# Three of four chunks of each down projection as seven products of quarters

## The chip, the cores and the metric

The kernel runs on one core of one Trainium2 chip, in one launch. The metric is the device time of one execution in microseconds. The core has five engines that run their own queues in strict order and wait for each other by semaphores: TensorE (PE, matrix products into PSUM), VectorE (DVE), ScalarE (ACT), GpSimd (POOL) and SyncE (SP, whose queue issues every DMA of this kernel).

## The reference

A trunk of two layers over 512 tokens with 1024 features: a token mixer, an MLP with 4096 hidden features, and a gated embedding, each added to the residual x. Only the MLP is touched:

```python
def sq_relu_mlp(h, w_up, w_down):
    return jnp.square(jax.nn.relu(h @ w_up)) @ w_down
...
        x = x + sq_relu_mlp(rmsnorm(x, mlp_norm[i]), w_up[i], w_down[i])
        gate = jax.nn.sigmoid(rmsnorm(x, ple_norm[i]) @ w_ple_gate[i])
        x = x + gate * (p[i] @ w_ple_proj[i])
    return rmsnorm(x, final_norm)
```

## The kernel before

Features lie on the 128 partitions and the 512 tokens (S) along the free axis, so x is 8 tiles of 128 x 512. Every operand of a product is held as two parts, hi (rounded to the matmul's type) and lo (the rest). mm3 (L161) makes a product from three matmuls, hi x hi, lo x hi and hi x lo (L163 to L165): in dense (L273) the weights are the stationary operand and the activations the moving one of 512 columns. split (L167) makes the two parts: ACT casts (L170), DVE subtracts (L171).

Weights come in blocks of 128 x 1024 in the order of _schedule, which is also their order in memory. fetch (L125) brings one: SP issues the DMA into a raw tile wr (L137), ACT casts it to wh (L138), DVE subtracts for wl (L139). The three tags have three buffers each, and load (L142) keeps two blocks ahead of PE. A cast into wh therefore waits until PE is done with the block three places earlier.

mlp (L643) goes through the hidden features in four chunks of 1024. An up projection of a chunk is 8 dense blocks (24 matmuls each, 8 tiles of the contraction x 3) whose results DVE takes through relu and the norm's row factor (L659), ACT squares (L660) and split makes into operands. A down projection of a chunk is again 8 dense blocks, one for each 128 output features, with the chunk's 8 hidden tiles as moving operands; residual (L285) adds each result to x. The up blocks of chunk c + 1 stand partly before and partly after the down blocks of chunk c. In the last chunk the norm of the gate takes each finished tile of x (nG.tile), which POOL adds up (L236).

A scheduler places the instructions of each engine by priority and by the buffers that it thinks free, so the order on an engine is not simply the order of the code. PSUM has eight banks; hf has 18 buffers of 128 x 512, ar has 24 of 128 x 1024, qk three of 128 x 4 x 416.

Of the kernel before, what the change touches and what calls it, by code (L numbers as in the profile page):

```python
# [15 lines left out]
F32 = mybir.dt.float32  # L16
# [7 lines left out]
P = 128  # L24
# [15 lines left out]
G_A, G_B, G_MLP, G_PLE, G_FIN, G_Q, G_KV, G_N = 0, 8, 16, 32, 48, 56, 58, 59  # L40


def _schedule():

    out = []
    for i in range(GH):
        out += [(("qkv", i, b), 1024) for b in range(4)]
        if i == 0:
            out += [(("v0", b), n * 320) for b, n in enumerate((3, 3, 2))]
    out += [(("woA1", m), 768) for m in range(8)]  # L50
    out += [(("woA2", 0), 1024), (("upk", 0), 1024), (("woA2", 1), 1024)]
    out += [(("upk", b), 1024) for b in range(1, 4)]
    out += _mlp_blocks(0)
    out += [(("win", b), 832) for b in range(4)]
    out += [((n, 0), c) for n, c in (("uq", 768), ("ukv", 512))]
    for g in range(1, 4):
        out += [((n, g), c) for n, c in (("uq", 768), ("ukv", 512))]
    out += [(("woB", h, b), 1024) for h in range(2) for b in range(4)]
    out += _mlp_blocks(1)
    return out  # L60


def _mlp_blocks(l):
# [12 lines left out]


@with_exitstack
def trunk(ctx: ExitStack, tc: tile.TileContext, xT, pT, cols, mask, tabs, wts, out):
# [36 lines left out]


    offs, order, o = {}, [], 0
    for key, n in _schedule():
# [5 lines left out]
    fetched = {}  # L125

    def fetch(key, pieces=1):

# [13 lines left out]
    def load(key, ahead=2):  # L142
        i = order.index(key)
        for j in range(i, min(i + 1 + ahead, len(order))):
            if order[j] not in fetched:
                run(fetch(order[j]))
        return fetched[key]


# [8 lines left out]
    rt = cp.tile([P, NT, 48], F32, name="rt")  # L158
    mk = unit(BF16, (P, 3, 256))

    def mm3(out_, l, r, first, last):  # L161

        T.matmul(out_, l[0], r[0], start=first, stop=False)  # L163
        T.matmul(out_, l[1], r[0], start=False, stop=False)  # L164
        T.matmul(out_, l[0], r[1], start=False, stop=last)  # L165

    def split(hi, lo, src, gain=None):  # L167

# [131 lines left out]
    def run(gen):  # L300
        for _ in gen:
            pass
# [338 lines left out]


    def mlp(l, nM, first=()):  # L643
        rb = [None]

        def up(c, b):
            ps = []
            for j in range(2):
                ps.append(dense(("up", l, c, 2 * b + j), KD, nM.k))
                if rb[0] is None and j == 0:  # L650
                    nM.columns()
            if rb[0] is None:
                rb[0] = nM.row()
            return up_out(ps)

        def up_out(ps):
            u = unit()
            for j in range(2):
                V.scalar_tensor_tensor(u[:, j * S:(j + 1) * S], ps[j], 0.0, rb[0], op0=ALU.max, op1=ALU.mult)  # L659
            A.activation(u, u, AF.Square)  # L660
            h, lo = unit(F32R), unit(F32R)
            split(h, lo, u)
            return [(h[:, j * S:(j + 1) * S], lo[:, j * S:(j + 1) * S]) for j in range(2)]

        nG = Norm(G_PLE + 8 * l)
        hid = []
        if first:
            nM.columns()
            ps = [dense(("up", l, 0, 4), KD, nM.k)]
            rb[0] = nM.row()  # L670
            hid += [up_out(first[:2]), up_out(first[2:])]
            ps.append(dense(("up", l, 0, 5), KD, nM.k))
            hid.append(up_out(ps))
        hid += [up(0, b) for b in range(len(hid), 4)]
        for c in range(NCH):
            flat = sum(hid, [])
            if c == NCH - 1:
                preload(AF.Sigmoid)
                pr = unit()
                nc.sync.dma_start(out=pr, in_=pT[:, l * 1024:(l + 1) * 1024])  # L680
                pe = unit(F32R), unit(F32R)
                split(*pe, pr)
            nxt = []
            if c + 1 < NCH:
                nxt.append(up(c + 1, 0))
            for m in range(KD):
                residual(m, dense(("down", l, c, m), KD, lambda k: flat[k]))
                if c == NCH - 1:
                    nG.tile(m)
            if c + 1 < NCH:  # L690
                nxt += [up(c + 1, b) for b in range(1, 4)]
            hid = nxt
        return nG, pe

    def embed(l, ph, pl):
# [398 lines left out]
def _arrange(inp):  # L1094
# [36 lines left out]
    def block(key):  # L1131
        n = key[0]
        if n == "qkv":
            i, b = key[1:]
            c = np.concatenate([hcol(*a, i) for a in ((0, 0), (1, 0), (0, 1), (0, 2), (1, 1), (1, 2), (2, 1), (2, 2))])
            return tiles(wq, slice(b * 256, (b + 1) * 256), c)
        if n == "v0":
            return tiles(wq, slice(key[1] * 384, min((key[1] + 1) * 384, D)), slice(1920, 1920 + GH * DH))
        if n == "woA1":
            return one(wo, 0, key[1])[:, [0, 1, 2, 3, 5, 6]]  # L1140
        if n == "woA2":
            return np.stack([one(wo, 0, 4 * key[1] + m)[:, [4, 7]] for m in range(4)], axis=1)
# [71 lines left out]
```

## Time and profile before

| | us |
|---|---|
| median of three runs | 1274.7 (1273.49 to 1274.9) |
| the profiled execution | 1275.82 |
| its span in the trace | 1274.0 |

| engine | busy, us | share of the span | instructions |
|---|---|---|---|
| PE | 1246.3 | 98% | 6224 |
| DVE | 738.3 | 58% | 1242 |
| ACT | 587.6 | 46% | 967 |
| POOL | 138.4 | 11% | 177 |

The span runs from the first instruction to the last; the device time has a little more around it. Matmuls are pipelined, so their durations overlap and their number times their duration is more than the span; how fast PE goes is read from the starts. Layer 0's MLP lies at about 250 to 580 us of the span, layer 1's at about 850 to 1200.

### The profile page before, as it was taken

How to read it: one execution, taken by the hardware profiler on the slowest of the kernel's cores; microseconds unless marked ns; L12 is line 12 of the kernel's file. 1: busy time of each engine (PE TensorE's matmuls, PEld its weight loads, DVE VectorE, ACT ScalarE, POOL GpSimd, SP SyncE). 2: the span in 40 equal slices, each digit the busy share in tenths (PEclk: the TensorE clock that was granted, in tenths of full speed). 3: DMA queues.
4: the chain of work that ended last, by engine and by line, in shares of the span. 5: the costliest groups of instructions: out<-in, count | busy, mean ns of one | idle time of the engine just before them, and what ended most of it. 6: DMA issues, size and time to landing. Idle time of an engine off the chain costs nothing.

```text
span 1274.0 us, 16149 instructions
## 1 busy us (share of the span) xinstructions
PE 1246.3 (98%) x6224; PEld 1053.0 (83%) x6224; DVE 738.3 (58%) x1242; ACT 587.6 (46%) x967; POOL 138.4 (11%) x177
## 2 busy tenths in 40 slices
PE   8999999999999999999989999999999999999996
PEld 6888878888888888888878888888888888888896
DVE  6567676753343443454878998864434434335477
ACT  5566654542231331344558887753313223224464
POOL 5000000000000000020234442220000000001200
PEclk9999999999999999999999999999999999999998
DMA  6111113222222222332211010123222222333252
GB/s 225 67 66 67 58 57 103 99 99 99 99 93 93 97 99 99 110 105 84 83 50 38 29 40 18 50 83 100 99 91 94 98 99 100 99 99 106 93 160 105
DMA packets 34348, 113.18 MB, mean 89 GB/s; under 512 B 4064, under 2 KB 4832, under 8 KB 34272
## 3 DMA queue, kind: packets, MB, share of 16 engines
q1 hardware_dynamic: 34272, 112.15, 26.3%
q8 instruction: 49, 0.80, 0.3%
q14 instruction: 27, 0.22, 0.1%
HBM read 110.04 MB, written 2.10 MB: 88 GB/s over the span
## 4 chain that ended last, share of the span: by engine, by line
PE 87%; DVE 6%; ACT 5%; issue 1%; DMA 0%; DVEq 0%; SPq 0%; ACTq 0%
PE ps L165 27%; PE ps L163 27%; PE ps L164 27%; PE ps L897 2%; DVE u L171 1%; ACT u L170 1%; PE ps L919 1%; PE ps L913 1%; DVE wl L139 1%; ACT wh L138 1%; ACT h L170 1%; ACT h L883 1%; DVE sm L882 1%; ACT qk L384 0%; PE ps L258 0%
## 5 line engine op out<-in xcount | busy, mean ns | idle before, releaser
L163 PE MATMUL ps<-u,wh 128*128 128x512 f32 (+1 forms) x1256 | 476.5, 379 | 2.4 <-ACT u L173 2.4
L165 PE MATMUL ps<-u,wh 128*128 128x512 f32 (+1 forms) x1256 | 475.5, 379 | 0.0
L164 PE MATMUL ps<-u,wl 128*128 128x512 f32 (+1 forms) x1256 | 475.3, 378 | 0.0
L138 ACT CAST wh<-wr 128x1024 fp32r<-128x1024 f32 (+4 forms) x213 | 215.5, 1013 | 512.1 <-PE ps L165 446.7
L139 DVE TENSOR_TENSOR wl<-wr,wh 128x1024 fp32r<-128x1024 f32 (+4 forms) x213 | 250.8, 1178 | 96.3 <-ACT wh L138 95.4
L163 PEld LDWEIGHTS ps<-u,wh 128*128 128x128 f32 x1256 | 236.4, 188 | 46.7 <-ACT u L173 3.0
L165 PEld LDWEIGHTS ps<-u,wh 128*128 128x128 f32 x1256 | 236.4, 188 | 45.1 <-DVE u L171 0.7
L164 PEld LDWEIGHTS ps<-u,wl 128*128 128x128 f32 x1256 | 236.5, 188 | 44.0
L285 DVE TENSOR_TENSOR x<-x,ps 128x512 f32<-128x512 f32 x96 | 65.7, 686 | 178.5 <-PE ps L165 177.6
L236 POOL TENSOR_TENSOR h<-h,h 128x512 f32<-128x512 f32 x24 | 39.2, 1634 | 769.5 <-ACT h L235 765.9
L659 DVE SCALAR_TENSOR_TENSOR u<-ps,h 128x512 f32<-128x512 f32 x64 | 43.8, 690 | 124.5 <-PE ps L165 124.5
L163 PE MATMUL ps<-wh,u 128*128 128x512 f32 (+4 forms) x272 | 102.1, 379 | 6.5 <-ACT wh L138 5.8
L171 DVE TENSOR_TENSOR u<-ps,u 128x512 fp32r<-128x512 f32 (+4 forms) x148 | 96.4, 665 | 16.0 <-ACT u L170 14.1
L164 PE MATMUL ps<-wh,u 128*128 128x512 f32 (+4 forms) x272 | 99.5, 368 | 0.0
L165 PE MATMUL ps<-wl,u 128*128 128x512 f32 (+4 forms) x272 | 98.8, 370 | 0.4 <-DVE wl L139 0.4
L170 ACT CAST u<-ps 128x512 fp32r<-128x512 f32 (+3 forms) x148 | 81.7, 573 | 29.2 <-PE ps L511 11.6
L163 PEld LDWEIGHTS ps<-wh,u 128*128 128x128 f32 x272 | 51.7, 191 | 12.4 <-ACT wh L138 6.0
L171 DVE TENSOR_TENSOR u<-u,u 128x1024 fp32r<-128x1024 f32 x34 | 41.7, 1225 | 30.6 <-ACT u L170 30.6
L165 PEld LDWEIGHTS ps<-wl,u 128*128 128x128 f32 x272 | 51.5, 190 | 7.7 <-DVE wl L139 1.3
L164 PEld LDWEIGHTS ps<-wh,u 128*128 128x128 f32 x272 | 51.8, 190 | 6.0 <-DVE u L174 0.3
L890 POOL TENSOR_SCALAR h<-h,sm 128x512 f32<-128x512 f32 x64 | 45.2, 707 | 99.8 <-DVE sm L889 90.0
L897 PE MATMUL ps<-ident,h 128*128 128x128 f32 x256 | 51.0, 272 | 0.5 <-ACT h L883 0.4
(161 smaller groups left out, 1330.5 us busy)
## 6 DMA issues: line engine op xcount, KB each, us to landing
wr<-wts SPq DMA_DIRECT2D x182, 512.0 KB, 3.3
wr<-wts SPq DMA_DIRECT2D x12, 384.0 KB, 3.1
wr<-wts SPq DMA_DIRECT2D x12, 256.0 KB, 5.0
x<-xT SPq DMA_DIRECT2D x8, 256.0 KB, 5.4
wr<-wts SPq DMA_DIRECT2D x4, 416.0 KB, 3.0
out<-u SPq DMA_DIRECT2D x6, 256.0 KB, 2.1
u<-pT SPq DMA_DIRECT2D x2, 512.0 KB, 4.6
wr<-wts SPq DMA_DIRECT2D x2, 480.0 KB, 5.0
```

Source lines behind the costliest of these rows:

```text
L138: A.copy(hi[:, c], raw[:, c])
L139: V.tensor_tensor(lo[:, c], raw[:, c], fl(hi[:, c]), op=ALU.subtract)
L163: T.matmul(out_, l[0], r[0], start=first, stop=False)
L164: T.matmul(out_, l[1], r[0], start=False, stop=False)
L165: T.matmul(out_, l[0], r[1], start=False, stop=last)
L170: a = A.copy(hi, src)
L171: v = V.tensor_tensor(lo, src, fl(hi), op=ALU.subtract)
L236: (V if self.n == KD - 1 else self.eng).tensor_tensor(self.acc, self.acc, sq, op=ALU.add)
L285: V.tensor_tensor(x[m], x[m], src, op=ALU.add)
L659: V.scalar_tensor_tensor(u[:, j * S:(j + 1) * S], ps[j], 0.0, rb[0], op0=ALU.max, op1=ALU.mult)
L890: return G.tensor_scalar(e, e, rl, 1.0, op0=ALU.mult, op1=ALU.mult)
L897: T.transpose(pt[:, tok(c)], e[:, tok(c)], ident)
```

## The change

For chunks 0 to 2 of each layer the down projection is no longer 8 dense blocks. The chunk's activations A (tokens x 1024 hidden) and its weights B (1024 hidden x 1024 features) are each cut into quarters, and the product is formed from seven products of quarters instead of eight, with sums that are shared (Strassen's scheme in Winograd's form):

- sums of weights (combine, L150 to L152): T1 = B12 - B11, T3 = B22 - B12, T2 = B22 - T1; and B21 - T2 (L170). Three quarters are loaded a second time for this, as halves of 128 x 512 (quarters, L145, 12 DMAs a chunk).
- sums of activations (left, L764 to L768): S3 = A11 - A21, S2 = A22 - S3, S4 = A12 - S2, S1 = A21 + A22. relu (L725) writes token half by token half, so that a quarter lies together.
- products: P1 = A11 B11, P2 = A12 B21, P6 = S2 T2, P5 = S1 T1, P7 = S3 T3, P3 = S4 B22, P4 = A22 (B21 - T2), in this order.

A product is two blocks (b = 0, 1) of 12 matmuls: two halves of 128 tokens x two tiles of the contraction x 3. The activations are now stationary and the weights move, so a result has tokens on the partitions and 512 features along the free axis. P1, P6, P7 and P4 accumulate in one pair of banks, P5 and P3 in another, P2 in a third; after each product put (L716, or a copy by ACT at L719 the first time) adds the bank to a store acc in SBUF, which takes the three buffers of qk. One up block of the next chunk follows each product (two the last). In chunk 3, which stays dense, four transposes (L840) turn each 128 x 512 piece of acc, and a second residual addition brings it to x. The 24 residual additions of chunks 0 to 2 of each layer go away.

The lines in the order rows and in the text are those of the kernel that they come from: mm3's matmuls are L163 to L165 before and L216 to L218 now, split is L170/L171 and L223/L224, fetch's cast and subtraction L138/L139 and L188/L189.

```diff
+PRODUCTS = (1, 2, 6, 5, 7, 3, 4)
...
 def _mlp_blocks(l):
...
+    out = [(("up", l, 0, m), 1024) for m in range(4 if l == 0 else 0, 8)]
+    for c in range(NCH - 1):
+        for n, p in enumerate(PRODUCTS):
+            out += [(("prod", l, c, p, b), 0) for b in range(2)]
+            out += [(("up", l, c + 1, m), 1024) for m in range(n, n + 1 if n < 6 else 8)]
+    out += [(("down", l, NCH - 1, m), 1024) for m in range(8)]
...
+    def quarters(l, c, k):
+        b, cs = k // 2, slice(k % 2 * S, (k % 2 + 1) * S)
+        sums[l, c, k] = [half() for _ in range(3)]
+        for t, q in zip(sums[l, c, k], (0, 1, 3)):
+            nc.sync.dma_start(out=t, in_=stored(("quarter", l, c, q, b))[:, cs])
+
+    def combine(l, c, k):
+        b11, b12, b22 = sums[l, c, k]
+        V.tensor_tensor(b11, b12, b11, op=ALU.subtract)
+        V.tensor_tensor(b12, b22, b12, op=ALU.subtract)
+        V.tensor_tensor(b22, b22, b11, op=ALU.subtract)
+
+    def fetch_prod(key):
+        _, l, c, p, b = key
+        if p in (1, 2, 3):
+            run(fetch(("quarter", l, c, {1: 0, 2: 2, 3: 3}[p], b)))
...
+        ts = [sums[l, c, 2 * b + j][{5: 0, 7: 1, 6: 2, 4: 2}[p]] for j in range(2)]
+        if p == 4:
+            raw = wp.tile([P, 1024], F32, tag="wr", name=nm("wr"))
+            nc.sync.dma_start(out=raw, in_=stored(("quarter", l, c, 2, b)))
+            for j, t in enumerate(ts):
+                cs = slice(j * S, (j + 1) * S)
+                V.tensor_tensor(raw[:, cs], raw[:, cs], t, op=ALU.subtract)
+            split(hi, lo, raw)
+        else:
+            for j, t in enumerate(ts):
+                cs = slice(j * S, (j + 1) * S)
+                split(hi[:, cs], lo[:, cs], t)
...
+        def put(r, i, n, ps):
+            a = acc[2 * r + i][n]
+            if (r, i, n) in written:
+                V.tensor_tensor(a, a, ps, op=ALU.add)
+            else:
+                written.add((r, i, n))
+                A.copy(a, ps)
...
+        def left(c, b):
+            u, v, r = us.pop((c, b)), us.pop((c, b + 2)), unit()
+            pair(("A", b, c), v)
+            f, g = slice(0, S), slice(S, 2 * S)
+            V.tensor_tensor(u[:, f], u[:, f], u[:, g], op=ALU.subtract)
+            V.tensor_tensor(r[:, f], v[:, g], u[:, f], op=ALU.subtract)
+            V.tensor_tensor(r[:, g], v[:, f], r[:, f], op=ALU.subtract)
+            pair(("S24", b, c), r)
+            V.tensor_tensor(u[:, g], u[:, g], v[:, g], op=ALU.add)
+            pair(("S31", b, c), u)
...
+        def prod(c, p):
+            g = {1: "a", 2: "b", 6: "a", 5: "c", 7: "a", 3: "c", 4: "a"}[p]
+            new = p in (1, 2, 5)
+            if new:
+                chain[g] = [bank(), bank()]
+            for b in range(2):
+                w = load(("prod", l, c, p, b))
+                for i in range(2):
+                    for k in (2 * b, 2 * b + 1):
+                        cs = slice(k % 2 * S, (k % 2 + 1) * S)
+                        mm3(chain[g][i], factor(c, p, k, i), (w[0][:, cs], w[1][:, cs]), new and k == 0, k == 3, True)
...
+        for m in range(KD):
+            pt = bank()
+            for t in range(NT):
+                T.transpose(pt[:, tok(t)], acc[t][m // 4][:, m % 4 * P:(m % 4 + 1) * P], ident)
+            residual(m, pt)
+            residual(m, dense(("down", l, NCH - 1, m), KD, lambda k: flat[k]))
+            nG.tile(m)
```

Where the instructions move is shown at two places. The first is layer 0, where its first up projection ends and the down work begins. DVE before: relu and split of the last hidden pair, then weights and residual additions of the down blocks in turn (u is a pair of hidden tiles, ps a bank).

```order
L659 SCALAR_TENSOR_TENSOR u_2641<-ps_2610,h_2517 128x512
L139 TENSOR_TENSOR wl_2683<-wr_2681,wh_2682 128x1024
L171 TENSOR_TENSOR u_2646<-u_2641,u_2645 128x1024
L659 SCALAR_TENSOR_TENSOR u_2711<-ps_2649,h_2517 128x512
L139 TENSOR_TENSOR wl_2722<-wr_2720,wh_2721 128x1024
L659 SCALAR_TENSOR_TENSOR u_2711<-ps_2680,h_2517 128x512
```

DVE now, at the same place (ps_2650 is the last up block of chunk 0; wl_2710 belongs to the second half of P1, wl_2716 to the first up block of chunk 1, wl_2734 to the first half of P2):

```order
L725 SCALAR_TENSOR_TENSOR u_2648<-ps_2650,h_2520 128x2x256
L151 TENSOR_TENSOR h_2600<-h_2601,h_2600 128x512
L189 TENSOR_TENSOR wl_2710<-wr_2708,wh_2709 128x1024
L768 TENSOR_TENSOR u_2535<-u_2535,u_2648 128x512
L152 TENSOR_TENSOR h_2601<-h_2601,h_2599 128x512
L224 TENSOR_TENSOR u_2685<-u_2648,u_2684 128x1024
L765 TENSOR_TENSOR u_2683<-u_2648,u_2535 128x512
L189 TENSOR_TENSOR wl_2716<-wr_2714,wh_2715 128x1024
```

The weights' low halves now stand behind sums of weights and of activations; L768 reads the squared pair u_2648. On ACT the squares of the hidden pairs stood between the casts of the weight blocks before:

```order
L138 CAST wh_2682<-wr_2681 128x1024
L660 ACTIVATE u_2641<-u_2641 128x1024
L170 CAST u_2645<-u_2641 128x1024
L138 CAST wh_2721<-wr_2720 128x1024
L138 CAST wh_2753<-wr_2752 128x1024
L660 ACTIVATE u_2711<-u_2711 128x1024
```

ACT now:

```order
L223 CAST u_2589<-u_2527 128x1024
L188 CAST wh_2715<-wr_2714 128x1024
L188 CAST wh_2733<-wr_2732 128x1024
L727 ACTIVATE u_2648<-u_2648 128x1024
L223 CAST u_2684<-u_2648 128x1024
```

The square of u_2648 stands behind the cast into wh_2733, whose buffer is that of wh_2652, the first half of P1. PE before, at that time, is in the first two up blocks of chunk 1, each 24 matmuls on one block of weights:

```order
L165 MATMUL ps_2649<-u_2386,wh_2612 128x512
L163 MATMUL ps_2680<-u_2239,wh_2651 128x512
L164 MATMUL ps_2680<-u_2239,wl_2652 128x512
L165 MATMUL ps_2680<-u_2240,wh_2651 128x512
L163 MATMUL ps_2680<-u_2239,wh_2651 128x512
```

PE now, after P1's first half (ps_2706 and ps_2707 are P1, ps_2755 the up block, ps_2782 and ps_2783 P2):

```order
L216 MATMUL ps_2706<-wh_2709,u_2531 128x512
L217 MATMUL ps_2706<-wh_2709,u_2532 128x512
L216 MATMUL ps_2707<-wh_2709,u_2531 128x512
L217 MATMUL ps_2707<-wh_2709,u_2532 128x512
L216 MATMUL ps_2755<-u_2239,wh_2715 128x512
L216 MATMUL ps_2782<-wh_2733,u_2577 128x512
L217 MATMUL ps_2782<-wh_2733,u_2578 128x512
L216 MATMUL ps_2783<-wh_2733,u_2577 128x512
L217 MATMUL ps_2783<-wh_2733,u_2578 128x512
L218 MATMUL ps_2706<-wl_2710,u_2531 128x512
```

Here the scheduler took matmuls that need only high halves ahead: nine of them stand before the first that reads wl_2710, and seven more of P1 follow that one before the rest of the up block, which begins with wl_2716.

The second place is the beginning of the last chunk's down blocks in layer 0. PE before goes from the last up block (ps_4218) straight to the first down block (ps_4265):

```order
L164 MATMUL ps_4218<-u_2385,wl_4190 128x512
L165 MATMUL ps_4218<-u_2386,wh_4189 128x512
L163 MATMUL ps_4265<-u_3787,wh_4220 128x512
L164 MATMUL ps_4265<-u_3787,wl_4221 128x512
L165 MATMUL ps_4265<-u_3788,wh_4220 128x512
```

PE now (ps_4463 is the last up block, ps_4508 the turned sum, ps_4514 the down block):

```order
L217 MATMUL ps_4463<-u_2385,wl_4418 128x512
L218 MATMUL ps_4463<-u_2386,wh_4417 128x512
L840 MATMUL ps_4508<-ident,acc_2464 128x128 x2
L840 MATMUL ps_4508<-ident,acc_2465 128x128
L840 MATMUL ps_4508<-ident,acc_2466 128x128
L216 MATMUL ps_4514<-u_4090,wh_4465 128x512
```

Four transposes stand ahead of each down block, and nothing else moved there on PE.

More of the change, by code (lines that the diff above doesn't have):

```diff
@@ L75, in _mlp_blocks, with _stored @@
     return out
+def _stored():
+    out = [e for e in _schedule() if e[1]]
+    return out + [(("quarter", l, c, q, b), 1024) for l in range(2) for c in range(NCH - 1)
+                  for q in range(4) for b in range(2)]
 @with_exitstack
@@ L159, in trunk, with mm3 @@
     mk = unit(BF16, (P, 3, 256))
[L161 to L165, printed above, removed]
+    def mm3(out_, l, r, first, last, more=False):
+        T.matmul(out_, l[0], r[0], start=first, stop=False, skip_group_check=more)
+        T.matmul(out_, l[1], r[0], start=False, stop=False, skip_group_check=more)
+        T.matmul(out_, l[0], r[1], start=False, stop=last, skip_group_check=more)
     def split(hi, lo, src, gain=None):
@@ L643, in mlp @@
     def mlp(l, nM, first=()):
+        H = S // 2
         rb = [None]
[L646 to L663, printed above, removed]
+        store = [qp.tile([P, NT, 416], F32, tag="qk", name=nm("acc")).rearrange("p t c -> p (t c)") for _ in range(3)]
@@ new lines, in halves, with up @@
+        def halves(u, j):
+            return u.rearrange("p (h j s) -> p h j s", h=2, j=2)[:, :, j, :]
+        us, ops, flat = {}, {}, []
+        def up(c, m, ps=None):
+            if ps is None:
+                ps = dense(("up", l, c, m), KD, nM.k)
+            if m % 2 == 0:
+                us[c, m // 2] = unit()
+            relu(c, us[c, m // 2], m % 2, ps)
+            if m % 2 == 0:
+                return
+            b = m // 2
+            if c == NCH - 1:
+                h, lo = unit(F32R), unit(F32R)
+                split(h, lo, us.pop((c, b)))
+                flat.extend((h[:, j * S:(j + 1) * S], lo[:, j * S:(j + 1) * S]) for j in range(2))
+            elif b < 2:
+                if b == 0:
+                    ops["A11", 0, c] = unit(F32R), unit(F32R)
+                cs = slice(b * S, (b + 1) * S)
+                split(*(t[:, cs] for t in ops["A11", 0, c]), us[c, b][:, :S])
+            else:
+                left(c, b - 2)
@@ L665, in mlp @@
         nG = Norm(G_PLE + 8 * l)
-        hid = []
         if first:
             nM.columns()
-            ps = [dense(("up", l, 0, 4), KD, nM.k)]
+            ps = dense(("up", l, 0, 4), KD, nM.k)
             rb[0] = nM.row()
[L671 to L692, printed above, removed]
+            for m in range(4):
+                up(0, m, first[m])
@@ new lines, in mlp @@
+            up(0, 4, ps)
+        else:
+            ps = [dense(("up", l, 0, 0), KD, nM.k)]
+            nM.columns()
+            ps.append(dense(("up", l, 0, 1), KD, nM.k))
+            rb[0] = nM.row()
+            for m in range(2):
+                up(0, m, ps[m])
+            for m in range(2, 5):
+                up(0, m)
+        for m in range(5, 8):
+            up(0, m)
+            if m == 5:
+                for k in range(4):
+                    quarters(l, 0, k)
+        for c in range(NCH - 1):
+            for k in range(2):
+                combine(l, c, k)
+            for n, p in enumerate(PRODUCTS):
+                prod(c, p)
+                if n < 2:
+                    combine(l, c, n + 2)
+                if p == 4 and c + 1 < NCH - 1:
+                    for k in range(4):
+                        quarters(l, c + 1, k)
+                for m in range(n, n + 1 if n < 6 else 8):
+                    up(c + 1, m)
@@ L1160, in block @@
             return one(down[l], c * D, m)
+        if n == "quarter":
+            l, c, q, b = key[1:]
+            r0 = c * D + q // 2 * 512 + b * 256
+            return tiles(down[l], slice(r0, r0 + 256), slice(q % 2 * 512, (q % 2 + 1) * 512))
         if n == "gate":
```

56 lines of the change are left out of this document (44 added, 12 removed).

## The prediction

> **What bounds the kernel now.** I read the page first: busy time, granted clock, the chain that ended last.
>
> ```profile
> span 1274.0 us, 16149 instructions
> ...
> PE 1246.3 (98%) x6224; PEld 1053.0 (83%) x6224; DVE 738.3 (58%) x1242; ACT 587.6 (46%) x967; POOL 138.4 (11%) x177
> ...
> PEclk9999999999999999999999999999999999999998
> ...
> PE 87%; DVE 6%; ACT 5%; issue 1%; DMA 0%; DVEq 0%; SPq 0%; ACTq 0%
> ```
>
> PE has work 98% of the span at full clock, and 87% of the chain is PE's. The change lies in the two MLPs, so I asked for stretches inside each (columns: PE, PEld, DVE, ACT, POOL busy, clock, DMA share, GB/s).
>
> ```profile
> 342.00:467.00 125.00, 125.00 (x554) 103.48 (x553) 53.85 (x54) 38.96 (x38) 0.00 (x0) 1.00 0.29 97
> 940.00:1020.00 80.00, 80.00 (x354) 66.28 (x353) 33.63 (x34) 23.85 (x23) 0.00 (x0) 1.00 0.29 93
> ```
>
> There PE never idles, while DVE is busy 43% and ACT 30%. A matmul fewer shortens the end, and work added to DVE and ACT is free until it makes PE wait. Matmuls overlap, so their price is the distance between starts, from PE's timeline; these rows are 24 matmuls apart.
>
> ```profile
> 340.03 0.39 PE L163 MATMUL ps<-u,wh 128*128 128x512 f32 x1
> ...
> 345.47 0.39 PE L163 MATMUL ps<-u,wh 128*128 128x512 f32 x1
> ```
>
> 5.44 us for 24, or 0.2267 us each, against a duration of 0.39.
>
> **Matmuls removed.** A down chunk was 8 blocks x 8 x 3 = 192 matmuls; seven products of 24 are 168. Six chunks lose 6 x 24 = 144: 144 x 0.2267 = 32.6 us. In the products the activations are stationary and the weights stream, which the first attention projection already does; these rows are 12 matmuls apart, first in a steady run, then between other work.
>
> ```profile
> 21.98 0.39 PE L163 MATMUL ps<-wh,u 128*128 128x512 f32 x1
> ...
> 24.70 0.39 PE L163 MATMUL ps<-wh,u 128*128 128x512 f32 x1
> ...
> 84.52 0.40 PE L163 MATMUL ps<-wh,u 128*128 128x512 f32 x1
> ...
> 87.27 0.39 PE L163 MATMUL ps<-wh,u 128*128 128x512 f32 x1
> ```
>
> 2.72 and 2.75 us. I take the first, the same pace as before, because the products run in steady stretches; by the second the 1008 remaining matmuls would cost 1008 x 0.0025 = 2.5 us more.
>
> **Transposes added.** The accumulated sum is turned in the last chunk, 8 x 4 per layer: 64 transposes, 16 groups of four. Four stand between matmuls in the trace:
>
> ```profile
> 257.06 0.39 PE L165 MATMUL ps<-u,wh 128*128 128x512 f32 x1
> ...
> 257.28 0.60 PE L211 MATMUL ps<-ident,sm 128*128 128x128 f32 x4
> ...
> 257.64 0.48 PE L163 MATMUL ps<-u,wh 128*128 128x512 f32 x1
> ...
> 257.95 0.39 PE L164 MATMUL ps<-u,wl 128*128 128x512 f32 x1
> ```
>
> The same operation by its own duration (min, median, max in ns), from the rows of the tile ident:
>
> ```profile
> L897 PE MATMUL ps<-ident,h x256: 270/272/328, 678.6 to 825.5; 128*128 128x128 f32 x128
> ```
>
> From the first matmul to the last is 0.89 us; two steps of 0.2267 belong to matmuls, so four transposes cost 0.44. 16 x 0.44 = 7.0 us on the path. The upper end is the duration of one, 0.272, with no overlap: 64 x 0.272 = 17.4. I take 7.0, since the row shows just this arrangement. The Trainium skill, "TensorE: Matmul & The Clock Gate", section "Part 4: PE-mode transpose", speaks against the change here: about 275 ns for a transpose in a kernel, which does not count as activity for the clock gate. By that, 64 x 0.275 = 17.6 us; this trace agrees on the duration but not on the cost in a stream, and its granted clock stays at 1.00 here.
>
> **DVE, ACT, DMA: covered on average.** Prices, by shape, and DVE's timeline for operations queued back to back:
>
> ```profile
> L139 DVE TENSOR_TENSOR wl<-wr,wh 128x1024 fp32r<-128x1024 f32 x182 | 222.8, 1224 | 90.8 <-ACT wh L138 90.1 <-PE ps L897 0.6
> ...
> L138 ACT CAST wh<-wr 128x1024 fp32r<-128x1024 f32 x182 | 191.9, 1055 | 495.9 <-PE ps L165 446.2 <-issue 40.9 <-ACT h L235 4.1
> ...
> L285 DVE TENSOR_TENSOR x<-x,ps 128x512 f32<-128x512 f32 x96 | 65.7, 686 | 178.5 <-PE ps L165 177.6 <-PE ps L634 0.5
> ...
> L659 DVE SCALAR_TENSOR_TENSOR u<-ps,h 128x512 f32<-128x512 f32 x64 | 43.8, 690 | 124.5 <-PE ps L165 124.5
> ...
> L171 DVE TENSOR_TENSOR u<-u,u 128x1024 fp32r<-128x1024 f32 x34 | 41.7, 1225 | 30.6 <-ACT u L170 30.6
> ...
> L660 ACT ACTIVATE u<-u 128x1024 f32<-128x1024 f32 x32 | 33.8, 1057 | 5.4 <-DVE u L659 5.4
> ...
> L236 DVE TENSOR_TENSOR h<-h,h 128x512 f32<-128x512 f32 x18 | 14.3, 794 | 0.5
> ...
> L724 DVE TENSOR_TENSOR h<-h,u 128x512 f32<-128x512 f32 x8 | 5.4, 685 | 0.1
> ...
> L170 ACT CAST h<-h 128x512 fp32r<-128x512 f32 x8 | 5.0, 621 | 0.9 <-DVE h L930 0.8
> ```
>
> ```profile
> 259.71 1.28 DVE L659 SCALAR_TENSOR_TENSOR u<-ps,h 128x512 f32<-128x512 f32 x2
> 263.20 1.23 DVE L171 TENSOR_TENSOR u<-u,u 128x1024 fp32r<-128x1024 f32 x1 [2.21 <-ACT u L170]
> 264.35 1.28 DVE L659 SCALAR_TENSOR_TENSOR u<-ps,h 128x512 f32<-128x512 f32 x2
> 265.54 1.21 DVE L139 TENSOR_TENSOR wl<-wr,wh 128x1024 fp32r<-128x1024 f32 x1
> ```
>
> Steady chunk, DVE: 22 operations on 1024 columns (8 up blocks, 6 plain and 2 subtracted product blocks, 6 splits in left) x 1.23 = 27.1; on 512 columns 8 relu, 12 halves of weight sums, 4 subtractions for product 4, 12 combines, 8 in left, 2 for A11, 14 puts = 60 x 0.69 = 41.4. Together 68.5 us in PE's 360 x 0.2267 = 81.6. ACT: 16 block casts, 4 squares, 6 splits x 1.06 and 14 halves x 0.62 = 36 us. Sums of two SBUF tiles are not in this stage before; their nearest rows are L724 at 0.685 and L236 at 0.794. I take 0.69, which also L285 and L659 show for a PSUM source; with 0.794 throughout DVE needs 74.7. Splitting a tile in two 256-column runs (relu's new output) has no row; I price it as L659. So nothing is bound on average, and I cost this work at nothing but where a queue delays weights; without the cover each microsecond beyond 81.6 would come six times. The last chunk's 8 further additions have 5.44 + 0.44 us a block to hide in. Products 6, 7 and 4 accumulate into a bank that DVE or ACT has read in between; three blocks, 16.3 us, lie between a bank's product and the next one that writes it, and a put takes 0.69, so PE does not wait for puts.
>
> DMA: per chunk 12 x 256 KB of quarters and 16 x 512 KB of blocks, 11.5 MB in 81.6 us, 141 GB/s; the first 20 us moved 304. On SP twelve quarter DMAs stand ahead of the next weight blocks: at 304 GB/s their 3.1 MB take 10.3 us, while three wr buffers let SP issue two to three blocks, 11 to 16 us, ahead of the cast that reads them.
>
> ```profile
> DMA packets 3447, 6.09 MB, mean 304 GB/s; under 512 B 636, under 2 KB 892, under 8 KB 3447
> ```
>
> ```profile
> wr<-wts SPq DMA_DIRECT2D x182, 512.0 KB, 3.3
> ...
> wr<-wts SPq DMA_DIRECT2D x12, 256.0 KB, 5.0
> ```
>
> **One wait added, opening layer 0.** The rows with the change show it. The up blocks keep their times: the block after 257.7 ends at 263.2, the others at 268.6 and 274.1; DVE's work on them starts at 259.7. Product 1's first half (12 matmuls) ends at 276.8. PE then has nine matmuls (2.0) and eight (1.8) before it needs wl_2716, at 280.7. That low half is late by a chain. ACT's cast into wh_2733 waits for the buffer that product 1's first half reads: 276.8 + 1.06 = 277.9. The square behind it ends at 278.9. DVE's L768 waits for that square: 279.6; one combine (0.60, half the distance 264.35 to 265.54), a split (1.15, 263.20 to 264.35) and L765 (0.60) follow, then wl_2716 itself (1.23): 283.2. PE waits 283.2 - 280.7 = 2.5 us; queued behind on PE are the rest of that up block and product 2, and wl_2734 is then in time. Ends: 0, if the casts and semaphores run a little closer than I add them and PE's 17 matmuls a little longer; and 3.6 if DVE's operations do not overlap. In that case the 20 operations on 512 and 5 on 1024 columns from 259.7 through wl_2710 end at 279.7 instead of 277.5 and are 0.9 late for PE, and the five after them (4.5) are 2.7 late again. Layer 1 has no four finished up blocks to catch up on when it opens: nothing.
>
> **Sum.** -32.6 + 7.0 + 2.5 = -23.1. The profiled execution took 1275.8 us (span 1274.0), so 1252.7; the median of three, 1274.7, lies 1.1 lower: 1251.6.
>
> **Rivals.**
> *Weights late in every chunk.* Each handoff is dense for DVE. From the end of the last up block: relu 0.69; the next up block's low half at 2.3 (its cast of 1.06 comes first); L768 3.0, a split 4.2, L765 4.8; product 2's first half 6.0; L766 6.6; two puts 7.8; two splits 10.3; product 2's second half 11.5. PE needs that at 5.44 + 5.44 + 2.72 and two matmuls, 14.05. So 2.5 us are left. For lateness speaks that ACT and DVE serve one strict order each, as in layer 0; against it this margin, which no other place in the chunk undercuts by my count. If all six chunks paid 2.5 us instead of one: 12.5 more, 1264.1. Chance 0.16.
> *Slower: quarters gate DVE.* Combines wait for DMAs into buffers that the previous chunk frees late (its P5, P7 and P4 weight sums), and behind such a combine DVE holds the relu, puts and the next wl, for which PE waits. A transfer lands in 3.3 to 5.0 us, about what DVE does between freeing a buffer and the combine that waits for its refill, and 2.5 us of margin come on top. There are four such handoffs (two per layer), so from 23.1 / 4 = 5.8 us lost at each the kernel is slower; with 7 us each, as when transfers of 3 MB pile up on SP's one queue ahead of a combine, 28 us are lost: 1279.6. Against: 141 GB/s is less than half of 304. Chance 0.05.
> *Transposes cost their duration.* 17.4 for 7.0: 1262.0. For it stands that each has to drain into the same bank as the next; four in 0.44 us speak against. Chance 0.06. The Trainium skill's section quoted with the transposes is on this rival's side.
> That the change leaves matmuls in place is excluded by the count of the order: 1008 for 1152.
>
> **How the numbers follow.** Forecast 0.70, rivals 0.16, 0.05, 0.06; 0.03 for a mixture that ends near no change. The forecast's own bounds: no opening wait gives 1249.1; 1.1 more wait and 2.5 of pace give 1255.2. The range goes 1 us below the first and up through most of the first rival's cases: 1248 to 1261. 0.2% is 2.5 us, about what a measurement can tell from no change. Faster 0.70 + 0.16 + 0.06 + 0.01 = 0.93, same 0.02, slower 0.05.
>
> **What would show it.** Right: PE busy in nearly all of each MLP, 24 product matmuls again 5.44 us apart, four acc transposes in about 0.44 us, one PE wait on wl of 2 to 3 us near 280 us, DVE about 80% busy in product chunks. Wrong: PE waits on wl or wh that repeat every chunk (the first rival's case or the quarters', told apart by what DVE waited for, ACT or DMA), or transposes a microsecond apart in fours.

## The result, and the profile after

| | before | after |
|---|---|---|
| median, us | 1274.1 | 1252.7 (1251.68 to 1253.96) |
| profiled execution, us | 1275.82 | 1251.68 |
| its span, us | 1274.0 | 1249.9 |

The ratio is 0.983 (95% interval 0.9815 to 0.9849): 21.4 us less by the medians, 24.1 by the two spans. The prediction had 23.1 less, and 1251.6 for the median. The page of the kernel after, its busy times and the chain that ended last:

```profile
PE 1220.9 (98%) x6144; PEld 1031.8 (83%) x6144; DVE 907.9 (73%) x1518; ACT 653.7 (52%) x1079; POOL 136.8 (11%) x177
...
PE 84%; DVE 8%; ACT 6%; issue 1%; DMA 0%; DVEq 0%; SPq 0%; ACTq 0%
```

PE is the bound as before and is busy 25 us less; DVE does 170 us more work, nearly all of it beside PE. Where the time went is read from a row that stands in each MLP's first up projection and again behind its down work: the four transposes of a norm's factor on PE. The prediction shows the first one before the change, at 257.28. Here are the other three from before, then all four from after:

```profile
601.63 0.60 PE L211 MATMUL ps<-ident,sm 128*128 128x128 f32 x4
...
863.40 0.60 PE L211 MATMUL ps<-ident,sm 128*128 128x128 f32 x4
...
1219.57 0.65 PE L211 MATMUL ps<-ident,sm 128*128 128x128 f32 x4 [0.55 <-DVE sm L203]
```

```profile
256.57 0.60 PE L264 MATMUL ps<-ident,sm 128*128 128x128 f32 x4
...
592.41 0.60 PE L264 MATMUL ps<-ident,sm 128*128 128x128 f32 x4
...
851.85 0.60 PE L264 MATMUL ps<-ident,sm 128*128 128x128 f32 x4
...
1195.37 0.65 PE L264 MATMUL ps<-ident,sm 128*128 128x128 f32 x4 [0.55 <-DVE sm L256]
```

From the first to the second row, layer 0's MLP takes 335.8 us instead of 344.4; from the third to the fourth, layer 1's takes 343.5 instead of 356.2. That is 8.5 and 12.7 us less, 21.2 together; the rest of the 24.1 lies outside the MLPs. The same two distances are used for the experiments below.

Stretches of two handoffs in layer 0 (PE, PEld, DVE, ACT, POOL busy, clock, DMA share, GB/s) and, from PE's timeline, a product's first matmul and the one 24 behind it:

```profile
299.00:380.00 81.00, 81.00 (x359) 67.05 (x359) 61.60 (x78) 37.69 (x46) 0.00 (x0) 1.00 0.44 143
380.00:462.00 82.00, 82.00 (x363) 67.91 (x362) 61.22 (x78) 34.51 (x40) 0.00 (x0) 1.00 0.38 125
```

```profile
299.27 0.39 PE L216 MATMUL ps<-wh,u 128*128 128x512 f32 x1
...
304.71 0.39 PE L216 MATMUL ps<-u,wh 128*128 128x512 f32 x1
```

PE has no idle time in either stretch, and 24 product matmuls take 5.44 us, as forecast. DVE is busy 61.6 of 81 us (76%), where the prediction counted 68.5 of 81.6. Two things make the difference: each of these stretches holds 78 of the 82 operations that it counted, and it priced them at their durations, while queued ones overlap (1.14 and 0.60 us from start to start, for 1.22 and 0.68). Four transposes, from the last matmul ahead of them to the second behind:

```profile
522.09 0.39 PE L218 MATMUL ps<-u,wh 128*128 128x512 f32 x1
522.32 0.60 PE L840 MATMUL ps<-ident,acc 128*128 128x128 f32 x4
522.67 0.48 PE L216 MATMUL ps<-u,wh 128*128 128x512 f32 x1
522.99 0.40 PE L217 MATMUL ps<-u,wl 128*128 128x512 f32 x1
```

0.90 us less two steps of 0.2267: 0.45 us a group, 0.44 forecast. The one wait that the prediction placed near 280 us is there. PE's timeline, then stretches with the clock (third number from the end; the last section says why they are cut there), then ACT's and DVE's timelines ahead of it:

```profile
282.32 0.56 PE L217 MATMUL ps<-u,wl 128*128 128x512 f32 x1 [2.12 <-DVE wl L189]
282.68 0.63 PE L218 MATMUL ps<-u,wh 128*128 128x512 f32 x1
...
286.07 0.40 PE L217 MATMUL ps<-u,wl 128*128 128x512 f32 x1
286.31 0.40 PE L218 MATMUL ps<-u,wh 128*128 128x512 f32 x1
```

```profile
279.21:282.62 3.41, 1.29 (x6) 0.78 (x5) 3.41 (x5) 2.22 (x3) 0.00 (x0) 1.00 0.31 124
282.62:286.04 3.42, 3.42 (x9) 2.64 (x8) 3.42 (x5) 1.99 (x2) 0.00 (x0) 0.50 0.72 195
```

```profile
276.05 1.05 ACT L188 CAST wh<-wr 128x1024 fp32r<-128x1024 f32 x1 [1.44 <-PE ps L217]
277.01 1.06 ACT L727 ACTIVATE u<-u 128x1024 f32<-128x1024 f32 x1
```

```profile
278.10 0.69 DVE L768 TENSOR_TENSOR u<-u,u 128x512 f32<-128x512 f32 x1 [0.57 <-ACT u L727]
...
281.05 1.22 DVE L189 TENSOR_TENSOR wl<-wr,wh 128x1024 fp32r<-128x1024 f32 x1
```

The chain is the predicted one: the cast waits for PE, the square stands behind it, L768 behind the square, wl at the end. PE idles 2.12 us (2.5 forecast). But then the clock is at 0.50 for 3.4 us, and from 282.68 to 286.07 the matmuls start 0.41 to 0.43 us apart. Ten steps from 282.32 to 286.31 would be 2.27 us at full pace and took 3.99. So the opening costs 2.1 + 1.7 = 3.8 us, more than the 3.6 given as its upper end; the prediction had priced the idle time alone.

### The profile page after: what moved, and what is told of

It is laid out like the page before. It is cut to its first block, busy times and chain, and to the rows that moved or that the text cites. A ratio compares the mean times of both kernels' runs of the same rounds, so it can differ in the third digit from the quotient of the medians.

```text
span 1249.9 us, 16595 instructions
## 1 busy us (share of the span) xinstructions
PE 1220.9 (98%) x6144; PEld 1031.8 (83%) x6144; DVE 907.9 (73%) x1518; ACT 653.7 (52%) x1079; POOL 136.8 (11%) x177
## 4 chain that ended last, share of the span: by engine, by line
PE 84%; DVE 8%; ACT 6%; issue 1%; DMA 0%; DVEq 0%; SPq 0%; ACTq 0%
PE ps L218 26%; PE ps L216 26%; PE ps L217 26%; PE ps L1048 2%; DVE wl L189 1%; DVE u L224 1%; PE ps L1070 1%; PE ps L1064 1%; DVE x L338 1%; ACT u L223 1%; ACT wh L188 1%; ACT h L223 1%; PE ps L840 1%; DVE sm L1033 1%; ACT h L1034 1%
## 5 line engine op out<-in xcount | busy, mean ns | idle before, releaser
L188 ACT CAST wh<-wr 128x1024 fp32r<-128x1024 f32 (+4 forms) x201 | 202.6, 1009 | 354.5 <-PE ps L218 265.8
L216 PE MATMUL ps<-u,wh 128*128 128x512 f32 (+1 forms) x872 | 329.1, 377 | 2.4 <-ACT u L226 2.4
L217 PE MATMUL ps<-u,wl 128*128 128x512 f32 (+1 forms) x872 | 326.5, 374 | 2.1 <-DVE wl L189 2.1
L218 PE MATMUL ps<-u,wh 128*128 128x512 f32 (+1 forms) x872 | 326.6, 375 | 0.3 <-DVE u L227 0.3
L189 DVE TENSOR_TENSOR wl<-wr,wh 128x1024 fp32r<-128x1024 f32 (+4 forms) x201 | 236.1, 1175 | 60.7 <-ACT wh L188 59.3
L216 PE MATMUL ps<-wh,u 128*128 128x512 f32 (+4 forms) x608 | 232.6, 384 | 6.6 <-ACT wh L188 5.9
L217 PE MATMUL ps<-wh,u 128*128 128x512 f32 (+4 forms) x608 | 230.0, 379 | 0.0
L218 PE MATMUL ps<-wl,u 128*128 128x512 f32 (+4 forms) x608 | 228.7, 380 | 0.4 <-DVE wl L189 0.4
L216 PEld LDWEIGHTS ps<-u,wh 128*128 128x128 f32 x872 | 164.7, 189 | 31.6 <-ACT u L226 3.0
L217 PEld LDWEIGHTS ps<-u,wl 128*128 128x128 f32 x872 | 164.8, 189 | 31.2 <-DVE wl L189 2.5
L218 PEld LDWEIGHTS ps<-u,wh 128*128 128x128 f32 x872 | 164.5, 189 | 30.1 <-DVE u L227 0.7
L216 PEld LDWEIGHTS ps<-wh,u 128*128 128x128 f32 x608 | 114.5, 189 | 25.8 <-ACT wh L188 6.4
L218 PEld LDWEIGHTS ps<-wl,u 128*128 128x128 f32 x608 | 114.4, 188 | 20.7 <-DVE wl L189 1.3
L217 PEld LDWEIGHTS ps<-wh,u 128*128 128x128 f32 x608 | 114.7, 189 | 18.9 <-DVE u L227 0.3
L224 DVE TENSOR_TENSOR u<-ps,u 128x512 fp32r<-128x512 f32 (+4 forms) x148 | 96.4, 665 | 15.6 <-ACT u L223 13.8
L725 DVE SCALAR_TENSOR_TENSOR u<-ps,h 128x512 f32<-128x512 f32 x64 | 43.5, 688 | 79.2 <-PE ps L218 79.1
L223 ACT CAST u<-ps 128x512 fp32r<-128x512 f32 (+3 forms) x148 | 81.7, 572 | 28.8 <-PE ps L564 11.5
L224 DVE TENSOR_TENSOR u<-u,u 128x1024 fp32r<-128x1024 f32 (+1 forms) x58 | 63.5, 1113 | 11.7 <-ACT u L223 11.6
L223 ACT CAST wh<-h 128x512 fp32r<-128x512 f32 x72 | 41.6, 619 | 43.0 <-PE ps L217 31.8
L223 ACT CAST u<-u 128x1024 fp32r<-128x1024 f32 (+1 forms) x58 | 54.7, 962 | 6.7 <-DVE u L766 5.7
```

Source lines behind the costliest of these rows:

```text
L188: A.copy(hi[:, c], raw[:, c])
L189: V.tensor_tensor(lo[:, c], raw[:, c], fl(hi[:, c]), op=ALU.subtract)
L216: T.matmul(out_, l[0], r[0], start=first, stop=False, skip_group_check=more)
L217: T.matmul(out_, l[1], r[0], start=False, stop=False, skip_group_check=more)
L218: T.matmul(out_, l[0], r[1], start=False, stop=last, skip_group_check=more)
L223: a = A.copy(hi, src)
```

## The experiments

All were timed beside the kernel before, whose medians lay at 1274.2 to 1274.6, so that their times are compared with each other too.

### Is the gain the count of matmuls?

```diff
-                for i in range(2):
+                for e, i in [(e, i) for e in range(1 + (p == 4)) for i in range(2)]:
...
-                    if b == 1:
+                    if b == 1 and e == (p == 4):
```

The down projection then holds product 4 twice.

> Product 4's 24 matmuls are issued twice in each of the six chunks, with the same operands; nothing is loaded or computed for it on other engines. First theory: the gain of the change is the count of matmuls times the distance of their starts, so 144 more cost 144 x 0.2267 = 32.6 us: 1285.3, which is 11 above the kernel before (transposes and the opening wait). Rival: part of the gain comes from elsewhere (weights that stream instead of being stationary, 48 residual additions fewer), and then the kernel with eight products stays at or below 1274.

Measured 1284.3, ratio 1.0077 (1.0065 to 1.0089): 31.6 above the kernel after, against 32.6, and slower than before. In the traces each layer's MLP takes 16.3 us longer than in the kernel after (352.2 and 359.8), which is just 72 x 0.2267. So seven products in place of eight are the gain; the layout and the residual additions saved do not make one without them.

### What does a transpose cost?

```diff
-            for t in range(NT):
+            for t in [0, 1, 2, 3] * 2:
                 T.transpose(pt[:, tok(t)], acc[t][m // 4][:, m % 4 * P:(m % 4 + 1) * P], ident)
```

> Each of the 64 transposes of the sum is made twice, into the same place. First theory: four of them cost 0.44 to 0.49 us of PE, as in the trace: 16 x 0.44 to 0.49 = 7.0 to 7.8 more, 1259.7 to 1260.5. Rival: a transpose costs its duration of 0.272 us, 64 x 0.272 = 17.4 more, 1270.1.

Measured 1259.7, 7.0 more, with a wide scatter (1258.1 to 1265.2) that its one trace, of the fastest execution, does not explain; none of these times reaches the rival's 1270.1. PE's timeline, with eight in place of four:

```profile
521.73 0.39 PE L218 MATMUL ps<-u,wh 128*128 128x512 f32 x1
521.96 1.03 PE L840 MATMUL ps<-ident,acc 128*128 128x128 f32 x8
522.75 0.48 PE L216 MATMUL ps<-u,wh 128*128 128x512 f32 x1
523.07 0.40 PE L217 MATMUL ps<-u,wl 128*128 128x512 f32 x1
```

1.34 us for 0.90: four more cost 0.44, and each layer's MLP takes 3.4 us longer (339.2 and 346.9) for 32 more. The rival with 0.272 each is out. The Trainium skill, "TensorE: Matmul & The Clock Gate", section "Part 4: PE-mode transpose", has the duration right; as a price in a stream of matmuls it would have been 2.5 times too much.

### What does the opening cost?

```diff
+def _after(l, c, n):
+    s = int((l, c) == (0, 0))
+    return range(n + s, n + s + 1 if n < 6 else 8)
...
             for n, p in enumerate(PRODUCTS):
+                if (l, c, n) == (0, 0, 0):
+                    up(c + 1, 0)
                 prod(c, p)
```

> In layer 0 one up block of the next chunk stands ahead of the first product instead of behind it; nothing else moves. First theory: the PE wait near 280 us is DVE's and ACT's queue at this one handoff, and it costs its 2.1 us of idle PE and also the 8 matmuls behind it that start 0.428 us apart instead of 0.227 (8 x 0.2 = 1.6). The block ahead gives DVE 5.44 us: both go, 1252.7 - 3.7 = 1249.0. Rival: only the idle time counts, 1250.6. Second rival: DVE is behind by more than a block and the wait only moves to the next weights, 1252.7.

Measured 1248.3 (1247.96 to 1251.99), ratio 0.980 (0.9787 to 0.9813). That is 4.4 less, nearer to 3.7 than to the 2.1 of idle time alone; but the interval reaches up to the rival's 1250.6. The traces decide: layer 0's MLP takes 331.8 us for 335.8, 4.1 less, layer 1's the same 343.5, and in the down work no PE wait and no stretch at half clock is left. The slow matmuls belong to the price of a wait.

### Where is DVE's margin: its load, or the handoff?

Two kernels add about the same work to DVE, one on the chain of a handoff and one away from it.

```diff
-            V.tensor_tensor(lo[:, c], raw[:, c], fl(hi[:, c]), op=ALU.subtract)
+            for _ in range(2 if key[0] in ("up", "quarter") else 1):
+                V.tensor_tensor(lo[:, c], raw[:, c], fl(hi[:, c]), op=ALU.subtract)
```

> DVE writes the low half of every weight block of the MLPs twice (up blocks and quarters): 14 more operations of 1.14 us in each product chunk, 16 us on top of the 62 that DVE is busy of 81.6. First theory: what counts is the chain at each handoff, which has 2.5 us of margin at product 2's second half by the prediction's count; three of the added operations lie in it, 3.4 us, so PE waits about 0.9 us in each of six chunks, and 2.3 more at layer 0's opening: 1252.7 + 5.4 + 2.3 = 1260.4. Rival: DVE's average alone counts, 78 of 81.6 us is still enough, and only the opening pays: 1255.0.

```diff
-            V.scalar_tensor_tensor(o_, in_(ps), 0.0, in_(rb[0]), op0=ALU.max, op1=ALU.mult)
+            for _ in range(n):
+                V.scalar_tensor_tensor(o_, in_(ps), 0.0, in_(rb[0]), op0=ALU.max, op1=ALU.mult)
...
-            relu(c, us[c, m // 2], m % 2, ps)
+            relu(c, us[c, m // 2], m % 2, ps, 5 if c and m < 6 else 1)
```

> DVE takes six of the eight up blocks that stand between the products five times through relu instead of once: 24 more operations at 0.60 us of DVE's time, 14.4 us in each of the six product chunks, nearly the 16 of the run with the low halves written twice, but none of them among the last two up blocks, where a handoff lies. First theory: DVE's load is free as long as it stays under PE's 81.6 us (62 + 14.4 = 76) and only the handoff's chain of weights and sums has little margin: 1252.7, no new PE waits. Rival: the load itself delays weights, and the time rises as with the low halves, to about 1272.

Measured 1272.5 and 1252.8. The same two stretches with relu five times, then the second of them with the low halves twice:

```profile
299.00:380.00 81.00, 81.00 (x359) 67.07 (x358) 76.84 (x106) 38.60 (x47) 0.00 (x0) 1.00 0.42 143
380.00:462.00 82.00, 82.00 (x364) 67.89 (x363) 74.55 (x102) 34.92 (x40) 0.00 (x0) 1.00 0.37 125
```

```profile
380.00:462.00 82.00, 80.82 (x356) 66.30 (x356) 74.65 (x92) 33.62 (x40) 0.00 (x0) 1.00 0.37 122
```

With relu five times DVE is busy 95% and 91%, and PE loses nothing; at the same 91%, with the work on the chain, PE loses 1.18 us. From PE's timeline with the low halves twice, at a handoff:

```profile
384.56 0.50 PE L219 MATMUL ps<-wl,u 128*128 128x512 f32 x1 [1.18 <-DVE wl L190]
```

Three operations of 1.14 us more in the chain and a wait of 1.18 (1.08 at the next handoff): by that, the margin at product 2's second half is an estimated 3.4 - 1.2 = 2.2 us. In the kernel after it can be read directly at the same handoff, from DVE's operation and PE's first matmul on its result:

```profile
369.45 1.22 DVE L189 TENSOR_TENSOR wl<-wr,wh 128x1024 fp32r<-128x1024 f32 x1
```

```profile
373.17 0.39 PE L218 MATMUL ps<-wl,u 128*128 128x512 f32 x1
```

The low half is done at 370.67 and read at 373.17: 2.5 us, as the prediction counted. The first theory had the mechanism and missed the size, 19.9 us for 7.7. It had left out layer 1's opening and one more wait of 1.56 us at 940 us, and above all layer 0's opening, where two waits with slow matmuls cost, by the starts, 7.4 us more than in the kernel after.

To see whether a block ahead mends that too, the same doubling on the kernel of the last experiment:

> The low halves of the MLP's weight blocks written twice again, but on the kernel with one up block ahead of the first product. First theory: of the 22 us that the doubled halves cost, 7.4 were layer 0's opening (its two waits and slow matmuls against one) and 11 the other handoffs, which stay: 1248.3 + 11 = 1259.3. Rival: the block ahead buys too little for the doubled halves, the opening still waits, and the time is above 1264.

Measured 1272.2, no better than without the block: the rival holds. PE's timeline at the opening, and the operation on DVE that ended its wait:

```profile
289.08 0.80 PE L226 MATMUL ps<-wl,u 128*128 128x512 f32 x1 [7.41 <-DVE wl L197]
```

```profile
287.81 1.21 DVE L197 TENSOR_TENSOR wl<-wr,wh 128x1024 fp32r<-128x1024 f32 x1
```

DVE works without a pause from 263.1 us until then, and this low half stands behind relus, sums and splits. The opening is a backlog: with the block ahead PE waits 7.41 us at once, without it 5.67 and 2.17. Why the block buys so little here was not taken apart.

### Do the quarters' transfers have room?

```diff
-            nc.sync.dma_start(out=t, in_=stored(("quarter", l, c, q, b))[:, cs])
+            for _ in range(2):
+                nc.sync.dma_start(out=t, in_=stored(("quarter", l, c, q, b))[:, cs])
```

> Each of the 72 quarter transfers for the sums of weights is made twice into the same buffer: 3.1 MB more in each product chunk, 14.7 MB or 180 GB/s instead of 141. First theory: the transfers have room, DVE's waits for them grow but PE's do not: 1252.7. Rival, the prediction's case in which quarters gate DVE: the combines come 5 to 10 us late at each of the four handoffs and PE waits for the weights behind them: 1270 to 1285.

Measured 1264.0, between the two. ACT's timeline and a stretch at layer 0's opening:

```profile
283.18 1.04 ACT L189 CAST wh<-wr 128x1024 fp32r<-128x1024 f32 x1 [5.02 <-DMA wr<-wts]
```

```profile
277.00:284.00 7.00, 0.35 (x2) 0.00 (x0) 5.49 (x8) 1.95 (x3) 0.00 (x0) 0.72 0.89 312
```

There the transfers run at 312 GB/s, and a weight block that SP issued behind the quarters lands 5 us late; PE waits 6.92 us with slow matmuls behind. Later it waits 0.29 us in layer 0, and 0.76, 0.30 and 2.23 in layer 1. Before the longest of these a combine on DVE waits for a quarter, and the low half behind it ends at 973.85:

```profile
970.29 0.69 DVE L151 TENSOR_TENSOR h<-h,h 128x512 f32<-128x512 f32 x1 [3.71 <-DMA h<-wts]
```

```profile
973.90 0.50 PE L218 MATMUL ps<-u,wl 128*128 128x512 f32 x1 [2.23 <-DVE wl L190]
```

So the prediction's slower rival has a real mechanism: at the opening through the weights' own transfers, and once in layer 1 just as described, through a combine. In the kernel after, at the transfers' own size, combines wait up to 2.50 us for quarters, and PE never waits for that.

### A place that the change did not touch

In the trace of before, DVE's timeline has an operation on 128x4 integers of 2.70 us, whose minimum is 0.16; below it POOL's timeline:

```profile
658.88 2.70 DVE L193 TENSOR_SCALAR sm<-sm 128x4 int32<-128x4 int32 x1
```

```profile
658.81 7.25 POOL L820 MEMSET u<- 32x1024 f32 x8
```

In the trace of after it takes 0.91, with the same memsets beside it:

```profile
649.58 0.91 DVE L246 TENSOR_SCALAR sm<-sm 128x4 int32<-128x4 int32 x1
...
652.29 0.90 DVE L924 TENSOR_SCALAR sm<-sm 128x2 f32<-128x2 f32 x1
```

A memset is 7.25 / 8 = 0.91, so DVE waits for three whole ones or for one; other runs here show two (1.80). In both traces it starts 0.07 us behind the first memset, so the count does not follow from its start; each kernel has one trace, and whether one kernel varies by itself is not shown. Both kernels got the memsets a stage earlier:

```diff
-    kts, qts = ([(unit(F32R), unit(F32R)) for _ in range(2)] for _ in range(2))
-    for t in sum(kts + qts, ()):
-        G.memset(fl(t[QW:]), 0.0)
...
+    kts, qts = ([(unit(F32R), unit(F32R)) for _ in range(2)] for _ in range(2))
+    for t in sum(kts + qts, ()):
+        G.memset(fl(t[QW:]), 0.0)
     z = qp.tile([P, NT, 416], F32, tag="qk", name="z")
```

> On the kernel with one up block ahead of the first product, the eight memsets that POOL makes for the second mixer's operands (0.91 us each, 7.25 together) are issued a stage earlier. In the trace of before a DVE operation on 128x4 integers beside them took 2.70 us, in the trace after the change 0.91, against a minimum of 0.16, and the TENSOR_SCALAR of 128x2 behind took 0.90. First theory: DVE waits for whole memsets there (three, or one), so this place costs by chance and has nothing to do with the change; with the memsets gone both operations take under 0.2 us and the time falls by about 1.5, from 1248.3 to 1246.8. Rival: the long operation has another cause and stays, 1248.3.

> The kernel before, with only the second mixer's eight memsets issued a stage earlier. First theory: the place where DVE waits for POOL's memsets belongs to both kernels, and the kernel before gains at least the 1.5 us that the kernel after gained, up to 3.3 when it had drawn three memsets (2.70 instead of 0.16, and 0.90 instead of 0.15): 1271.1 to 1272.9. Rival: the kernel before has another place for this wait and gains nothing, 1274.4.

Measured 1246.9 (1246.07 to 1247.17) and 1271.6 (1270.45 to 1272.91), 1.5 and 2.7 less. In the first, DVE's timeline has both operations short:

```profile
644.82 0.17 DVE L253 TENSOR_SCALAR sm<-sm 128x4 int32<-128x4 int32 x1
646.80 0.17 DVE L936 TENSOR_SCALAR sm<-sm 128x2 f32<-128x2 f32 x1
```

So 1.8 of the 24.1 us between the two traces is this place and not the change. The Trainium skill, "SBUF — State Buffer", section "Who interferes with whom", says that VectorE in a two-port mode and GpSimd lock each other out for whole instructions; the steps of 0.91 us agree, though no run shows which mode this operation is in.

### The fourth chunk as products too

```diff
-        for c in range(NCH - 1):
+        for c in range(NCH):
...
+                if c + 1 == NCH:
+                    if p == 4:
+                        for m in (4, 5, 6, 7):
+                            turn(m)
+                    continue
```

In this kernel product 6's second half in the fourth chunk takes one sum of weights ahead of its last subtraction, so it waits for less there.

> The fourth chunk's down projection as seven products too, on the kernel with the block ahead and the early memsets (1246.9); the sum is then turned behind the last product, the second half of the features ahead of the first. 48 matmuls fewer in both layers together, 48 x 0.2267 = 10.9 us. First theory: the margin at a handoff, about 2 us by the doubled low halves, holds because an up block of 5.44 us stands between the first two products; without one PE waits about 3.4 us there, and about 2 more for the last sums before they can be turned, twice: 1246.9 - 10.9 + 10.8 = 1246.8, nothing gained. Rival: the sums and weights come in time without the up blocks as well, 1236 to 1238.

Measured 1256.4, 9.5 slower than without, and for another reason than the theory's. From PE's timeline at the end of layer 0's MLP (layer 1 has the same two waits):

```profile
566.48 0.80 PE L223 MATMUL ps<-u,wh 128*128 128x512 f32 x1 [6.12 <-ACT u L230]
...
570.06 0.79 PE L225 MATMUL ps<-u,wh 128*128 128x512 f32 x1 [1.51 <-DVE u L231]
```

The embedding's operand is split behind the residual additions, which a dense chunk had covered. The next kernel moves that split, turns half of the features earlier and makes every sum in its place:

```diff
+                    if n == 0:
+                        combine(l, c, 2)
+                        combine(l, c, 3)
+                    if n == 2:
+                        pr = unit()
...
+                        split(*pe, pr)
...
+                if b == 1 and p == 4 and c + 1 == NCH:
+                    for m in (4, 5, 6, 7):
+                        turn(m)
```

> The fourth chunk as products, with other work over its end: the embedding's operand is split two products earlier instead of behind the residual additions, the second half of the features is turned between the halves of product 4, the embedding's matmuls stand over the rest, and all sums of weights are made ahead of product 2. In the run before, PE waited 6.1 and 1.5 us in layer 0 for that operand, with slow matmuls behind, and nowhere in the chunk's products. First theory: those waits were all that ate the gain, and 48 matmuls fewer now show: 1246.9 - 10.9 + 0 to 3 = 1236 to 1239. Rival: at the handoff without up blocks the weights are late once the sums are made in their place, 3 to 5 us in each layer: 1242 to 1246.

Measured 1244.1, ratio 0.976 (0.9751 to 0.9778): the fastest here, but 2.8 below the kernel with three chunks, not 8 to 11. Neither theory's place waits: no weights are late. PE waits 2.44 us in each layer for the last sums of the store, and in layer 1 also 2.56 us for the norm behind (0.54 in the kernel with three chunks). PE's timeline for both, then DVE's and POOL's timelines in layer 0:

```profile
563.55 0.66 PE L829 MATMUL ps<-ident,acc 128*128 128x128 f32 x4 [2.44 <-DVE acc L723]
...
1186.51 0.97 PE L271 MATMUL ps<-ident,sm 128*128 128x128 f32 x4 [2.56 <-DVE sm L263]
```

```profile
558.90 2.32 DVE L196 TENSOR_TENSOR wl<-wr,wh 128x1024 fp32r<-128x1024 f32 x1
...
564.01 1.21 DVE L196 TENSOR_TENSOR wl<-wr,wh 128x1024 fp32r<-128x1024 f32 x1
```

```profile
557.13 5.21 POOL L296 TENSOR_TENSOR h<-h,h 128x512 f32<-128x512 f32 x3 [351.40 <-ACT h L295]
```

Ahead of those sums, DVE's subtraction takes 2.32 us beside POOL's additions and 1.21 without them. Layer 0's MLP takes 3.0 us less than with three chunks, 5.4 less 2.4 of waiting. In layer 1 the two waits and the 3.4 us at half clock behind each of them eat all of its 5.4 and 2.1 more. Of the 2.5 us between the two traces only 1.0 thus lies in the MLPs and the embeddings behind them. What the crowding on DVE beside POOL adds to these waits, and what the lost cover of the end, was not taken apart.

## Why the prediction was right

**Matmuls.** 32.6 us for 144: doubling one product cost 31.6 by the medians and 16.3 in each layer by the traces. **Transposes.** 7.0 forecast; doubling them cost 7.0 by the medians, which scatter widely, and 3.4 in each layer by the traces. **Opening.** The place, the chain and the idle time were right (2.5 for 2.1); the term was short by the 1.7 us of half clock behind the wait. **DVE, ACT, DMA at nothing.** Right: the load was lower than counted and PE waits for none of it at the handoffs.

The sum with the measured opening is -32.6 + 7.0 + 3.8 = -21.8; the two MLPs became 21.2 us shorter and the medians moved by 21.4. Layer 1, which has no opening wait, shows it best: -16.3 + 3.5 = -12.8 by the prediction's terms, 12.7 measured. The interval of the ratio spans a gain of some 19 to 24 us, so the medians alone could not tell 21.8 from the 23.1 of the forecast; the traces can. That 1251.6 lay only 1.1 below the result is in part luck: the kernel before came out 0.6 us faster than in the median that the prediction started from. The spans differ by more, 24.1: the part between the MLPs took 2.3 us less, 1.8 of it because DVE waited for three memsets in the trace of before and for one in that of after, and the part ahead of them 0.7.

**The rivals.** Weights late in every chunk did not happen; the margin that spoke against it is 2.5 us in the trace, as counted. Quarters that gate DVE did happen on a small scale, up to 2.50 us a combine, but never reached PE; twice the transfers did. Transposes at their duration are ruled out.

## What to carry to other kernels

Where one engine is busy all the time at a steady pace, price a change by the distance between its starts, and look for waits only where the order of the other engines changes hands: there a chain of a few operations decides, and average load said nothing here, up to 95%. Price a wait of the bound engine with what follows it, and look for places that vary from trace to trace before reading 2 us out of two traces. A scheme that saves work at its end also takes cover away there.

## What the runs showed of the hardware

**The clock after a gap.** A gap of 2.12 us halved PE's granted clock for 3.4 us, and gaps of 2.0 to 2.2 at the same place of three other kernels (product 4 twice, transposes twice, relu five times) were followed by the same slow steps; in the MLPs gaps of 1.1 to 1.6 us behind steady work were not, nor was one of 2.23 (twice the transfers). Two gaps of 2.44 us at the same place of the two layers in the last kernel went both ways (clock third from the end):

```profile
562.05:565.46 3.41, 1.91 (x13) 1.76 (x14) 3.41 (x5) 0.00 (x0) 0.29 (x1) 1.00 0.43 154
565.46:568.88 3.42, 3.42 (x17) 2.82 (x16) 3.35 (x5) 3.02 (x6) 1.59 (x1) 1.00 0.45 153
...
1162.80:1166.21 3.41, 0.97 (x6) 0.51 (x5) 3.41 (x4) 0.00 (x0) 1.97 (x1) 1.00 0.43 148
1166.21:1169.62 3.41, 3.41 (x13) 2.91 (x12) 3.41 (x6) 1.32 (x3) 0.00 (x0) 0.50 0.28 72
```

The traces say why. In every one the granted clock, once it has come to 1.00, changes only at whole steps of 3.413 us from there: in the kernel after it is 1.00 for 273.07 us, which is 80 steps, then 0.50 for one. The stretches above are cut at these steps. The gap in layer 0 lies across a cut, with 0.95 us before it and 1.50 behind; the gap in layer 1 lies within one step. The others fit: the gap of 2.23 is cut into 1.25 and 0.98, and the 2.12 of the kernel after lies in one step. Over the MLPs of all traces, each step at full clock with 1.87 us or more of idle PE was followed by one at 0.50, and none with 1.53 or less was. What lies between is not shown there.

The Trainium skill, "TensorE: Matmul & The Clock Gate", section "Part 1: The HAM clock gate", tells of windows of about 3.4 us that run freely; the steps of 3.413 us agree, but here 1.87 us of idle PE in one were enough.

**DVE beside POOL.** A DVE operation on four columns waited for whole memsets of 0.91 us, one to three of them in different traces, and a subtraction of two SBUF tiles took 2.32 us for 1.21 beside POOL's additions.
